# A hybrid MLA, SSD and RWKV kernel: one ct tile more, one h tile fewer, and RWKV row sums as single fp32 products

## The chip, the cores and the metric

The kernel runs on one core of a Trainium2 chip. The metric is the device time of one execution in microseconds (us); lower is better. Five engines work side by side, each through its own instructions in order: TensorE (PE; its weight loads are PEld), VectorE (DVE), ScalarE (ACT), GpSimd (POOL) and SyncE (SP, which here issues the DMAs). They wait for each other through semaphores.

## The reference

Two layers of a sequence model, batch 1, 1024 tokens of width 1024, fp32. Each layer normalises x with adaLN scale and shift, projects it to 4,680 columns, and feeds three branches: latent attention (MLA, 4 heads), a state space branch (SSD, 8 heads) and RWKV-7 (8 heads of 64). Their outputs are concatenated, projected and added to x under a gate.

```python
def reference(...):
    c_act = jax.nn.silu(c)
    for l in range(DEPTH):
        mod = c_act @ ada_w[l] + ada_b[l]
        shift, scale, gate = jnp.split(mod[:, None, :], 3, axis=-1)
        h = rms_norm(x, norm_w[l]) * (1.0 + scale) + shift
        (q_lat, ..., r, k, v, w_lo, a_lo, g_rwkv) = split_cols(h @ w_in[l], IN_SPLIT_SIZES)
        y_mla = mla_branch(...) * jax.nn.silu(g_mla)
        y_ssd = ssd_branch(...)
        y_rwkv = rwkv7_branch(...) * jax.nn.silu(g_rwkv)
        y = jnp.concatenate([y_mla, y_ssd, y_rwkv], axis=-1)
        x = x + gate * (y @ w_out[l])
    return rms_norm(x, final_norm_w)
```

In the RWKV branch two sums run over the 64 columns of each head, for every token:

```python
    kk = k * heads(k_k)
    kk = kk / jnp.maximum(jnp.sqrt(jnp.sum(kk * kk, axis=-1, keepdims=True)), 1e-12)
    ...
    y = y + jnp.sum(r * k * r_k.astype(f32), axis=-1, keepdims=True) * v
```

## The kernel before

Activations lie with features on the 128 partitions and 512 tokens (a half) along a row. A layer and a half make one stage: dense stages 0 to 3 are layer 0 half 0, layer 0 half 1, layer 1 half 0, layer 1 half 1. A dense stage makes h (make_h, L671) and projects it, 37 tiles of 128 columns (inproj, L705). For layer 1 it begins with the output projection of layer 0 (outproj, L1412), which also gives the new x; after the last stage two more output projections follow. Behind each dense stage come its consumers (L1625): RWKV in four head pairs, SSD, and attention.

Precise products are made of three reduced ones (fp32r): weights and activations are each split in a high and a low part, high in ScalarE, low in VectorE, and the products high-high, high-low and low-high are added up (split_w L534, split L1216, proj L692). A split activation takes two h tiles, a pair. Weights come through wr, wh and wl tiles.

Two tile pools matter here. **h** (N_H2 = 18 tiles of 128 x 512) holds x, the split h of a dense stage (8 pairs, 16 tiles), and in an output projection the 8 x tiles that are summed up and the split y tiles of a group. An output projection has three groups, one for each branch (y_split, L1403: 4 pairs a group). **ct** (N_CT = 4) holds what passes through: a y tile on its way from DRAM to its split (`ct<-yd`), an evacuated projection (evac L711, and L1430 in the first group), and rows of the adaLN matrix of the next layer (`ct<-in_ada_dram`, ada L610), which VectorE multiplies by the activated condition and adds up (`ac<-ct,cact,ac`, L631).

What sets the order is a planner. All instructions are recorded first (record, L257); order (L286) then places them with a table of costs and latencies: of those that could start, the one with the highest rank, which is what `plan.ahead` adds. The adaLN multiply-adds have rank 0 (PR_S, L61), their loads a high one (PR_L, L62), y loads and weight loads a high one (PR_D), and the consumers lie between. Tiles of a pool go to users in recorded order as they come free. The planner prices a product of at most 64 output rows at a fixed 103 ns (L230). So a change of a pool's size or of an instruction moves instructions on all engines.

The RWKV row sums: each head pair has one for the norm of kk (L788, two output rows, one for each head) and one for r k r_k (L834, 128 output rows). The left operand, bones, is 1 where two rows belong to the same head. With PQ = PB = 1 the squares (sq) or products (r) are split into fp32r parts in the tiles leafh and leafl, taken from the pool of b tiles, and two fp32r products with bones_r, a rounded copy of bones, are added up.

Of the kernel before, what the change touches and what calls it, by code (L numbers as in the profile page):

```python
# [10 lines left out]
F32R = mybir.dt.float32r  # L11
I32 = mybir.dt.int32
AF = mybir.ActivationFunctionType
# [4 lines left out]
P = 128  # L18
# [25 lines left out]
C_ID, C_MD, C_SM, C_BO, C_IF, C_SG, C_S4, C_M1 = 0, 128, 256, 768, 896, 897, 898, 902  # L44
NCST = 1030

N_H2, N_RT, N_RI, N_RQ, N_RL, N_CT, N_WR, N_WL, N_WH, N_B2 = 18, 5, 2, 2, 3, 4, 3, 3, 3, 17
N_BK, N_GG, N_BX, N_AR, N_BM, N_TT, N_RV, N_GT = 1, 2, 3, 1, 1, 2, 2, 2
RW_T = 0
N_EZ = 1  # L50
# [21 lines left out]
SG0 = "bbgggggg"  # L72
SBP, SBC, SCH = "ra", "ra", 2
SRB = "tf"
PQ = 1
PB = 1
PX = "b2"
WAT = "rv"
LOT = "rl"
# [318 lines left out]
def hybrid_layers_kernel(ctx: ExitStack, tc: tile.TileContext, A, out):  # L398
    nc = tc.nc
    plan = Plan(tc)  # L400
    V, S, G, PE, SP = (plan.engine(e, q) for e, q in ((nc.vector, "V"), (nc.scalar, "S"), (nc.gpsimd, "G"),
                                                      (nc.tensor, "P"), (nc.sync, "Q")))
    TQ, AL, AS, BL, BM, BS, EQ = SP, S, S, S, SP, S, SP

    cpool = ctx.enter_context(tc.tile_pool(name="cpool", bufs=1))
# [46 lines left out]
    def s1(n, tag=None, bufs=None):  # L452
        if bufs:
            return sm.tile([P, n], F32, name=nm("s"), tag=tag or f"s{n}", bufs=bufs)
        return sm.tile([P, n], F32, name=nm("s"), tag=tag or f"s{n}")

    def bank(tag):
        return ps.tile([P, HT], F32, name=nm("ps"), tag=tag, bufs=PSB[tag])
# [22 lines left out]
    bones = cst[:, C_BO:C_BO + 128]  # L481
# [17 lines left out]
    for e in range(2):  # L499
        SP.dma_start(cst[64:128, C_MD + 64 * e:C_MD + 64 * e + 64], A["cst"][64:128, C_MD + 64 * (1 - e):C_MD + 64 * (1 - e) + 64])  # L500
    SP.dma_start(mD1[64:128], A["cst"][64:128, C_MD:C_MD + 128])
    bones_r = cpool.tile([P, 128], F32R, name="bones_r")
    S.activation(bones_r, bones, AF.Copy)
    cth = s1(8)
    S.activation(cth, craw, AF.Tanh, scale=0.5)
    V.scalar_tensor_tensor(cth, cth, 1.0, craw, op0=ALU.add, op1=ALU.mult)
# [248 lines left out]
    def rwkv_a1(d, U, p, wa):  # L755
# [32 lines left out]
        pq = bank("ra")  # L788
        if PQ:
            hi, lo = WATS[PX](dt=F32R, leaf="leafh"), WATS[PX](dt=F32R, leaf="leafl")  # L790
# [13 lines left out]
    def rwkv_a2(d, p, u):  # L804
# [29 lines left out]
        pbn = bank("ra")  # L834
        if PB:
            hi, lo = WATS[PX](dt=F32R, leaf="leafh"), WATS[PX](dt=F32R, leaf="leafl")
# [917 lines left out]
```

## Time and profile before

| | |
|---|---|
| three runs | 1953.89 us median (1953.27 to 1957.49) |
| profiled execution | 1953.58 us, its span 1951.8 us |
| granted TensorE clock, mean | 0.975 |
| PE, DVE, ACT, POOL busy | 1825.9, 1619.7, 1205.9, 204.4 us |
| DMA | 341 MB, 175 GB/s |

A profile row groups instructions by line, engine, operation and tiles; every instruction is issued from L396, so rows are told apart by their tiles. `out<-in` names what is written and what is read, without buffer numbers. A product of plain fp32 operands makes two records of MATMUL, one of fp32r operands makes one. "Idle" in brackets is the engine's wait before an instruction, with what ended it. The granted clock is TensorE's share of its full rate (1.0 is 2.4 GHz, 0.5 is 1.2 GHz).

### The profile page before, as it was taken

Reading aid. Unit: us, or ns where it says so; the run is one execution under the profiler, and the core shown is the slowest. Engines: PE = TensorE matmul, PEld = TensorE weight load, DVE = VectorE, ACT = ScalarE, POOL = GpSimd, SP = SyncE. Lnnn points to the kernel's source line nnn. Section 1 sums busy time; section 2 is a strip of 40 time slices with the busy share of each in tenths; the row PEclk is TensorE's granted clock in tenths of the full one; section 3 lists DMA queues with packets and bytes.
Section 4 is the critical chain, followed back from the end, with each engine's and each line's share of the span. In section 5 each row is a group of like instructions: output and inputs, shape, how many; then the busy total and the mean of one; then the engine's idle time right before and its main releaser. Section 6 shows DMA issues by size and latency. Waiting matters only on the chain. (4 is left out here: it accounts for less than half of the span.)

```text
span 1951.8 us, 32300 instructions
## 1 busy us (share of the span) xinstructions
PE 1825.9 (94%) x10220; PEld 1460.7 (75%) x10220; DVE 1619.7 (83%) x4002; ACT 1205.9 (62%) x2520; POOL 204.4 (10%) x302
## 2 busy tenths in 40 slices
PE   5899997999999986989999999998999999999996
PEld 3677775888887764777778778787777877888884
DVE  7898898789897999787788978888788896978774
ACT  5566566676665655566657567675656557675652
POOL 2120011011010101020100001002010020001001
PEclk9999998999999986999999999999999999999997
DMA  7677666765658673744464665854456565753542
GB/s 248 219 201 200 182 198 190 225 200 164 190 152 212 195 205 102 238 132 114 122 165 133 157 203 171 272 170 141 131 146 177 157 203 171 246 162 100 183 144 73
DMA packets 273371, 341.31 MB, mean 175 GB/s; under 512 B 79152, under 2 KB 132016, under 8 KB 273200
## 3 DMA queue, kind: packets, MB, share of 16 engines
q1 hardware_dynamic: 273200, 339.25, 59.6%
q8 instruction: 81, 1.33, 0.3%
q14 instruction: 90, 0.74, 0.1%
HBM read 254.67 MB, written 84.47 MB: 174 GB/s over the span
## 5 line engine op out<-in xcount | busy, mean ns | idle before, releaser
L396 PE MATMUL ps<-h,wh 128*128 128x512 f32 x3136 | 1015.9, 407 | 35.3 <-ACT h L396 21.4
L396 PEld LDWEIGHTS ps<-h,wh 128*128 128x128 f32 x3136 | 581.2, 191 | 166.3 <-ACT h L396 26.8
L396 PE MATMUL ps<-h,wl 128*128 128x512 f32 x1568 | 590.1, 407 | 0.1
L396 PE MATMUL ps<-b,b 128*128 128x512 f32 (+4 forms) x1512 | 384.6, 356 | 10.5 <-DVE b L396 6.3
L396 ACT ACTIVATE wh<-wr 128x512 fp32r<-128x512 f32 (+1 forms) x398 | 246.4, 620 | 211.4 <-PE ps L396 164.3
L396 PEld LDWEIGHTS ps<-h,wl 128*128 128x128 f32 x1568 | 296.8, 191 | 56.7 <-issue 2.5
L396 DVE TENSOR_TENSOR wl<-wr,wh 128x512 fp32r<-128x512 f32 (+1 forms) x398 | 269.7, 680 | 59.4 <-ACT wh L396 41.1
L396 PEld LDWEIGHTS ps<-b,b 128*128 128x128 f32 (+1 forms) x1512 | 232.1, 184 | 67.6 <-DVE b L396 14.5
L396 ACT ACTIVATE b<-b 128x512 f32<-128x512 f32 (+3 forms) x222 | 136.9, 625 | 62.1 <-DVE b L396 25.6
L396 ACT ACTIVATE b<-ps 128x512 f32<-128x512 f32 (+3 forms) x201 | 99.4, 508 | 77.8 <-PE ps L396 73.6
L396 DVE TENSOR_TENSOR b<-b,b 128x512 fp32r<-128x512 f32 (+4 forms) x178 | 121.9, 690 | 18.4 <-ACT b L396 14.5
L396 DVE TENSOR_TENSOR rq<-rq,tmp 128x60 f32<-128x60 f32 (+24 forms) x496 | 109.1, 220 | 6.6
L396 DVE TENSOR_TENSOR tmp<-Q,rq 128x60 f32<-128x60 f32 (+24 forms) x496 | 104.3, 210 | 5.9
L396 ACT ACTIVATE ct<-ps 128x512 f32<-128x512 f32 x150 | 87.8, 588 | 24.1 <-PE ps L396 11.2
L396 PE MATMUL ps<-cst,b 128*128 128x128 f32 x452 | 81.6, 282 | 20.7 <-POOL b L396 15.0
L396 PEld LDWEIGHTS ps<-bx,gg 128*128 128x128 f32 x512 | 76.8, 194 | 32.2 <-DVE bx L396 15.8
L396 POOL COPY halo<-ct 128x3 f32<-128x3 f32 x84 | 28.6, 340 | 621.9 <-ACT ct L396 594.2
L396 PE MATMUL ps<-bx,gg 128*128 128x64 f32 x512 | 80.7, 273 | 9.2 <-DVE bx L396 7.6
L396 PEld LDWEIGHTS ps<-cst,b 128*128 128x128 f32 x452 | 58.4, 146 | 35.1 <-POOL b L396 15.0
L396 POOL TENSOR_TENSOR s<-s,nhalf 128x4 f32<-128x4 f32 (+1 forms) x34 | 54.0, 1591 | 258.1 <-DVE s L396 250.5
L396 DVE SCALAR_TENSOR_TENSOR h<-ps,md,h 128x512 f32<-128x512 f32 x72 | 53.5, 746 | 33.2 <-PE ps L396 32.7
L396 ACT ACTIVATE b<-ps,s,s 128x512 f32<-128x512 f32 (+2 forms) x96 | 63.9, 667 | 27.3 <-DVE s L396 24.3
(196 smaller groups left out, 2612.0 us busy)
## 6 DMA issues: line engine op xcount, KB each, us to landing
wr<-in_w_in_dram SPq DMA_DIRECT2D x282, 256.0 KB
U<-ct SPq DMA_DIRECT2D x84, 257.5 KB
wr<-in_w_out_dram SPq DMA_DIRECT2D x80, 256.0 KB
U<-ct SPq DMA_DIRECT2D x64, 256.0 KB
ct<-in_ada_dram SPq DMA_DIRECT2D x64, 256.0 KB
ri<-U SPq DMA_DIRECT2D x52, 257.5 KB
b<-accd SPq DMA_DIRECT2D x96, 128.0 KB
ct<-yd SPq DMA_DIRECT2D x48, 256.0 KB
```

What stands on the lines that cost most here:

```text
L396: o.fn(*o.args, **o.kw)
```

## The change

N_H2 goes from 18 to 17 and N_CT from 4 to 5. PQ and PB go from 1 to 0: the row sums are one plain fp32 product each, straight from sq or r with bones, without leafh, leafl and bones_r.

```diff
-N_H2, N_RT, N_RI, N_RQ, N_RL, N_CT, N_WR, N_WL, N_WH, N_B2 = 18, 5, 2, 2, 3, 4, 3, 3, 3, 17
+N_H2, N_RT, N_RI, N_RQ, N_RL, N_CT, N_WR, N_WL, N_WH, N_B2 = 17, 5, 2, 2, 3, 5, 3, 3, 3, 17
...
-PQ = 1
-PB = 1
+PQ = 0
+PB = 0
...
-    bones_r = cpool.tile([P, 128], F32R, name="bones_r")
-    S.activation(bones_r, bones, AF.Copy)
```

What the switch chooses between, in rwkv_a1 (rwkv_a2 has the same with r, bones and 128 output rows):

```python
        if PQ:
            hi, lo = WATS[PX](dt=F32R, leaf="leafh"), WATS[PX](dt=F32R, leaf="leafl")
            split(sq, hi, lo)
            mm(pq[0:2, :], bones_r[:, 0:128:64], hi, stop=False)
            mm(pq[0:2, :], bones_r[:, 0:128:64], lo, start=False)
        else:
            mm(pq[0:2, :], bones[:, 0:128:64], sq)
```

The order moves on every engine. The places below lie in the output projection of layer 0, half 0, at the change from its first group of y tiles (SSD) to its second (attention). First VectorE before: `h<-ct,h` is the low part of a y split, `ac<-ct,cact,ac` an adaLN multiply-add, rq, tmp and Q belong to the inversion of an RWKV matrix.

```order
L396 SCALAR_TENSOR_TENSOR h_2429<-ct_2427,h_2428 128x512
L396 TENSOR_TENSOR tmp_1807<-Q_1802,rq_1806 128x60
L396 SCALAR_TENSOR_TENSOR ac_1638<-ct_2394,cact,ac_1638 128x512
L396 TENSOR_TENSOR rq_1806<-rq_1806,tmp_1807 128x10x6
L396 SCALAR_TENSOR_TENSOR ac_1638<-ct_2401,cact,ac_1638 128x512
L396 TENSOR_TENSOR tmp_1807<-Q_1802,rq_1806 128x54
L396 SCALAR_TENSOR_TENSOR ac_1638<-ct_2408,cact,ac_1638 128x512
```

The multiply-adds of the last three adaLN rows stand behind the third split of the group (h_2429). VectorE in the changed kernel, from the first split of the same group (h_2390) to its last (h_2399):

```order
L396 SCALAR_TENSOR_TENSOR h_2390<-ct_2388,h_2389 128x512
L396 TENSOR_TENSOR rq_1777<-rq_1777,tmp_1778 128x19x4
L396 TENSOR_TENSOR wl_2410<-wr_2408,wh_2409 128x512
L396 TENSOR_TENSOR h_2379<-h_2379,ct_2381 128x512
L396 SCALAR_TENSOR_TENSOR h_2393<-ct_2391,h_2392 128x512
L396 TENSOR_TENSOR tmp_1778<-Q_1773,rq_1777 128x72
L396 TENSOR_TENSOR bm_1787<-bm_1787,s_1792 128x512
L396 SCALAR_TENSOR_TENSOR h_2396<-ct_2394,h_2395 128x512
L396 TENSOR_TENSOR rq_1777<-rq_1777,tmp_1778 128x18x4
L396 TENSOR_TENSOR wl_2415<-wr_2413,wh_2414 128x512
L396 SCALAR_TENSOR_TENSOR h_2399<-ct_2397,h_2398 128x512
```

The four splits stand close together, and the adaLN multiply-adds of this half all stand ahead of them. SP's queue, which issues the loads (yd is a y tile in DRAM), before:

```order
L396 DMA ct_2408<-in_ada_dram 128x512
L396 DMA b_2038<-rope_d 128x512
L396 DMA b_2039<-rope_d 128x512
L396 DMA wr_2461<-in_w_out_dram 128x512
L396 DMA ct_2421<-yd_583 128x512
L396 DMA b_2055<-in_w_q_dram 128x512
L396 DMA ct_2424<-yd_584 128x512
L396 DMA ct_2427<-yd_585 128x512
```

And in the changed kernel, where the last load of adaLN rows of that half is ct_2375:

```order
L396 DMA ct_2375<-in_ada_dram 128x512
L396 DMA qn_1998<-b_2028 128x512
L396 DMA ct_2388<-yd_582 128x512
L396 DMA wr_2413<-in_w_out_dram 128x512
L396 DMA ct_2391<-yd_583 128x512
L396 DMA qn_1999<-b_2033 128x512
L396 DMA b_2047<-in_w_v_dram 128x512
L396 DMA qn_2000<-b_2035 128x512
L396 DMA ct_2394<-yd_584 128x512
L396 DMA wr_2418<-in_w_out_dram 128x512
L396 DMA ct_2397<-yd_585 128x512
```

In the queue the two kinds of load stand in the same sequence; what moved is when VectorE frees the tiles that they wait for.

## Rows read from the trace of the kernel before

**Rows 1.** The page: busy us (share of the span) and instructions of each engine.

```profile
PE 1825.9 (94%) x10220; PEld 1460.7 (75%) x10220; DVE 1619.7 (83%) x4002; ACT 1205.9 (62%) x2520; POOL 204.4 (10%) x302
```

**Rows 2.** Busy time by stretch: start:end, length, each engine's busy us (records).

```profile
core 0: us, PE busy (x) PEld busy (x) DVE busy (x) ACT busy (x) POOL busy (x), PEclk, DMA share, GB/s
0.00:310.70 310.70, 271.81 (x1369) 210.30 (x1369) 267.44 (x660) 189.36 (x397) 45.74 (x71) 0.99 0.70 208
310.70:690.50 379.80, 360.53 (x2132) 291.60 (x2132) 330.46 (x854) 240.21 (x512) 37.21 (x66) 0.98 0.68 191
690.50:877.80 187.30, 156.85 (x876) 122.87 (x877) 163.67 (x388) 111.96 (x222) 22.40 (x23) 0.89 0.55 168
877.80:1951.80 1074.00, 1036.69 (x5846) 835.97 (x5844) 858.13 (x2102) 664.42 (x1391) 99.06 (x144) 0.98 0.55 161
...
80.00:310.70 230.70, 221.58 (x1172) 175.63 (x1170) 200.61 (x477) 144.96 (x289) 27.39 (x45) 0.99 0.73 206
335.00:675.00 340.00, 335.96 (x2023) 273.45 (x2022) 295.22 (x778) 222.68 (x478) 32.22 (x58) 0.99 0.68 190
735.00:785.00 50.00, 31.54 (x116) 22.17 (x114) 44.02 (x122) 29.04 (x55) 8.48 (x7) 0.69 0.34 105
```

**Rows 3.** Timeline of SP, 690 to 785 us: start, us, engine, out<-in, count.

```profile
710.67 0.33 SPq L396 DMA_DIRECT2D ct<-in_ada_dram  x1
721.04 0.33 SPq L396 DMA_DIRECT2D ct<-in_ada_dram  x1
748.41 0.33 SPq L396 DMA_DIRECT2D ct<-in_ada_dram  x1
755.92 0.32 SPq L396 DMA_DIRECT2D ct<-yd  x1
762.32 7.62 SPq L396 DMA_DIRECT2D ct<-yd  x2
776.80 0.42 SPq L396 DMA_DIRECT2D ct<-yd  x1
```

**Rows 4.** Timeline of VectorE, 735 to 792 us.

```profile
761.61 0.68 DVE L396 SCALAR_TENSOR_TENSOR h<-ct,h 128x512 fp32r<-128x512 f32 x1
768.90 0.68 DVE L396 SCALAR_TENSOR_TENSOR h<-ct,h 128x512 fp32r<-128x512 f32 x1
775.17 0.68 DVE L396 SCALAR_TENSOR_TENSOR h<-ct,h 128x512 fp32r<-128x512 f32 x1
775.91 0.74 DVE L396 SCALAR_TENSOR_TENSOR ac<-ct,cact,ac 128x512 f32<-128x512 f32 x1
776.71 0.74 DVE L396 SCALAR_TENSOR_TENSOR ac<-ct,cact,ac 128x512 f32<-128x512 f32 x1
777.91 0.74 DVE L396 SCALAR_TENSOR_TENSOR ac<-ct,cact,ac 128x512 f32<-128x512 f32 x1
```

**Rows 5.** Timeline of TensorE, 728 to 792 us: idle before it in brackets.

```profile
767.55 0.57 PE L396 MATMUL ps<-h,wh 128*128 128x512 f32 x1 [3.31 <-ACT h L396]
769.64 0.79 PE L396 MATMUL ps<-h,wh 128*128 128x512 f32 x1 [1.52 <-DVE h L396]
```

**Rows 6.** Groups by form: busy us, mean ns | idle before; what the change removes.

```profile
L396 DVE TENSOR_TENSOR leafl<-rt,leafh 128x512 fp32r<-128x512 f32 x32 | 22.0, 687 | 2.5 <-ACT leafh L396 2.1
L396 ACT ACTIVATE leafh<-rt 128x512 fp32r<-128x512 f32 x32 | 20.0, 626 | 3.0 <-DVE rt L396 2.6
L396 PE MATMUL ps<-leafh,bones_r 128*128 128x512 f32 x16 | 6.9, 430 | 0.4 <-ACT wh L396 0.4
L396 PE MATMUL ps<-leafh,bones_r 128*2 128x512 f32 x16 | 6.8, 427 | 0.0
```

**Rows 7.** Timeline of TensorE, 1900 to 1908 us: starts of back-to-back products.

```profile
1902.36 1.09 PE L396 MATMUL ps<-h,wh 128*128 128x512 f32 x4
1903.28 0.40 PE L396 MATMUL ps<-h,wl 128*128 128x512 f32 x1
...
1905.34 0.59 PE L396 MATMUL ps<-b,b 128*128 128x256 f32 x2
1905.77 0.27 PE L396 MATMUL ps<-cst,b 128*128 128x128 f32 x1
```

**Rows 8.** Groups by form: small fp32 products, two records each.

```profile
L396 PE MATMUL ps<-rq,ar 32*32 32x32 f32 x512 | 18.7, 193 | 0.0
L396 PE MATMUL ps<-gg,bk 128*128 128x128 f32 x512 | 72.2, 283 | 8.1 <-DVE bk L396 3.5 <-ACT bx L396 2.6 <-issue 0.8
```

## Prediction

> **What bounds the kernel now.** I read the page's busy shares first: TensorE is busy 94% of the span, VectorE 83%, ScalarE 62% [rows 1]. Shares over a whole program hide its stages, so the next view is the busy time in four stretches that the program's own landmarks cut [rows 2]. A ends where VectorE begins to normalise the x of dense stage 1 (310.7 us). B is dense stage 1 with the work of the first two consumers. C runs from the first split y tile of layer 0's output projection (690.5 us) to the first normalised tile of layer 1 (877.8 us). D is the rest. In B and D TensorE works 95% and 97% of the time; from 335 to 675 us it is 336.0 of 340 us. There time is TensorE's work, and what the other engines do is cover. C is the exception: 156.9 busy of 187.3 us, the granted clock 0.89, and in its middle (735 to 785 us) 31.5 of 50 us at a granted 0.69. So 30.5 us of C are idle TensorE, and part of the rest ran at the lower of the two clock levels. The projection products are there to fill C; why don't they?
>
> The DMA queue and VectorE in that stretch say why [rows 3, 4]. SP issued adaLN rows into ct tiles at 710.67, 721.04 and 748.41 us. The multiply-adds that read them (ac<-ct,cact,ac) have the lowest rank and ran at 775.91, 776.71 and 777.91 us. Three of four ct tiles lay locked. The y tiles of the projection's second group went through the one that was left: issued at 755.92, split at 761.61 to 762.29, the next issued at 762.32, split at 768.90 to 769.58, the next after that, split at 775.17. Each y tile waits until the one before has been read: 6 to 7 us a turn. TensorE waits for it: 3.31 us for ScalarE's h and 1.52 us for VectorE's [rows 5].
>
> **The change, part by part.** *Row sums.* Each of the 32 removes one ScalarE copy (0.626 us), one VectorE subtract (0.687 us) and two fp32r products of 512 columns, and adds one plain fp32 product of 512 columns [rows 6]. Four fp32r products back to back start 0.92 us apart (1902.36 to 1903.28), 0.23 each; a plain fp32 product of 256 columns is two records and takes 0.43 us to the next start (1905.34 to 1905.77) [rows 7]. By columns 512 take 0.86. The 2-column sums cost as much as the 128-column ones (427 against 430 ns [rows 6]). So a sum costs 0.86 - 0.46 = 0.40 us more of TensorE: 32 x 0.40 = 12.8 us, of which 30 sums, 12.0 us, lie outside C in the new order. The bounds are 0 (all of them in idle time) and 12.8; B, D and the part of A that has sums (80 to 310.7 us: 221.6 of 230.7 us busy [rows 2]) are nearly full, so I take the upper. The 20.0 us of ScalarE and 22.0 us of VectorE that go [rows 6] are counted at nothing outside C, since TensorE's own work hides them; it shortens the chain copy, subtract, product, product by about a microsecond a head pair, which counts where TensorE waits. If it were TensorE that had slack, this part alone would be a gain.
>
> Beside that, from a page: the Trainium skill (FP8 and Floating Point Precision, TensorE Precision Notes) says that true fp32 takes four passes through the array. By that a sum would cost 4 x 0.23 = 0.92 and 32 of them 14.7 us more instead of 12.8; the row (0.43 for half the columns) is a little under it. It speaks against the change.
>
> *One ct tile more.* It gives C's ring a second free tile while three are locked, so a load can be under way while the tile before is split. The new order goes further: the adaLN multiply-adds stand ahead of the second group's splits (first and second order pieces), so that the locked tiles are free again too. Between the first and last split of that group VectorE had 47 instructions; now 10. In the whole of C VectorE has 294 instructions where it had 387, TensorE 624 where it had 696, with the same projection work (291 products against 288).
>
> What C then needs: VectorE 294 x 163.67/387 = 124 us [rows 2]. TensorE 156.85 us now, less the small products that moved out, less what it lost to the clock. The moved ones are 138 records, 64 of them of the 32 x 32 kind (18.7/512 = 0.037 us); the 128 x 128 kind has 0.141 [rows 8]: bounds 5 and 19 us, and I take 7, near the small kind. The clock: a mean of 0.69 over 735 to 785 us is 62% of it at half rate; that share of 31.5 busy us is 20, which at full rate would be 10. So TensorE needs 157 - 7 - 10 = 140 us, and with 4% idle (B and D have 5 and 3%) C takes 146 us. The bounds are 130 (VectorE's 124 with the same idle) and 180 (187.3 - 7, nothing gained).
>
> *One h tile fewer.* An output projection holds 8 x tiles and 8 split y tiles; of 18 two were left, a whole split pair ahead, and of 17 one. At each change of group (nine in the four projections) the second tile of a pair may have to wait. The nearest rows are the split itself, 0.68 us on VectorE [rows 4], and the wait for a late pair, 3.31 us [rows 5]; the lower bound is nothing, as the new order puts three of that group's four splits within 7 instructions. I take 0 at the point and keep 9 x 0.68 = 6 us for the range. The x loads of stage 1 are all but one issued after the H tiles come free; before, all but two: one load more of 0.4 us issue at 310 us, nothing.
>
> *The sum*, against the profiled execution (span 1951.8, 1953.6 in all, 0.3 under the median): A, B and D 1951.8 - 187.3 = 1764.5; plus sums 12.0; plus the work moved out of C 7.0; plus C 146; that is 1929.5, and 1.8 us around the span: **1931 us**.
>
> **Rivals.** *VectorE paces B and C.* It is busy 494 of their 567 us [rows 2], and its share in C is higher than TensorE's. For it: if VectorE was the limit, freeing ct tiles gives TensorE nothing to do sooner. Against it: TensorE waited for a split whose tile had not been loaded. In the new order the two stretches hold 1187 VectorE instructions instead of 1240; 53 x 0.40 = 21 us less, the sums cost 12.8 on TensorE outside: 1953.6 + 12.8 - 21 = 1945.
>
> *The change doesn't do what it says: the fifth tile fills with adaLN rows too.* The loads run ahead as far as tiles allow, eight in a row for a half, and their readers stay last in rank. Then C keeps its 187 us, the sums are paid in full, and the time is 1953.6 + 12.8 = 1966, slower. For it: the same rule of ranks; against it: the place of the multiply-adds in the new order. C has to shrink by more than 12.8 us before there is any gain; that is the point from which it decides.
>
> *The h pool opens the gap that the ct pool closed.* At every group change TensorE waits for the second tile of the pair. At 2.5 us a change (between 0.68 and 3.31) nine cost 22: 1931 + 22 = 1953, no change; above 2.9 us each it is slower. The Trainium skill (Perfetto Trace Analysis, Optimization Strategy) reads the same gap repeating on the engine that should be full as too few buffers; C's gaps of 6 to 7 us fit it for ct, and for h no repeated gap is in these rows. Its result would be this rival's.
>
> **How the numbers follow.** A measurement of this kernel tells about 0.2%, 4 us, from no change. The forecast, C between 130 and 166 us, 0.58; VectorE paces, 1945, 0.15; the ring stays locked, 1966, 0.18; the h gap, 1953, 0.09. Faster is the forecast and most of the second: 0.71; slower the third and part of the fourth: 0.22; the rest, 0.07, within 0.2%. The range: low with C at 130, 1764.5 + 19 + 130 + 1.8 = 1915, a little lower for small gains elsewhere, 1912; the high end takes in the second and fourth rival and reaches into the third, 1962. The forecast's own range is 1913 to 1949.
>
> **What would show it.** Right: in the trace after, 32 pairs of plain fp32 records at 0.43 us a record; TensorE's work up by about 13 us; C at 135 to 160 us with a granted clock near 0.97; y loads of the second group issued within some 5 us instead of 21; the wait for ScalarE's h there gone. Wrong: C as long as before, with adaLN rows lying in four tiles; or gaps of 2 to 3 us in front of split pairs at each group change; or VectorE above 95% over B with TensorE idle in front of the first y tile. A sum at 0.46 us (two passes a product) would put 12 us more on the gain.

## The result, and the profile after

The changed kernel takes 1939.07 us (median of four, 1937.37 to 1940.78) against 1954.22 of the kernel before beside it: 0.9923 of the time, interval 0.9901 to 0.9945. The forecast was 1931 us in a range of 1912 to 1962. So the time fell as forecast, by 15 us instead of 23. The page's first line, against [rows 1]:

```profile
PE 1828.5 (94%) x10220; PEld 1446.4 (75%) x10220; DVE 1593.1 (82%) x3970; ACT 1190.4 (61%) x2487; POOL 202.0 (10%) x302
```

The span fell from 1951.8 to 1937.4 us. TensorE is busy 2.6 us longer, and idle 108.9 us instead of 125.9, so in this count the whole gain is idle time that went. (The busy time holds two changes that nearly cancel: by the prediction's estimates the sums add 12.8 us, and the fuller clock in C gives back 10.) Where the idle time went is read from the same four stretches as in [rows 2], cut at the same landmarks (start:end, length, each engine's busy us and records, then granted clock, DMA share, GB/s); the last row is the same 50 us as in [rows 2]:

```profile
0.00:321.30 321.30, 280.95 (x1390) 213.96 (x1390) 272.15 (x673) 191.26 (x397) 47.16 (x74) 0.99 0.69 207
321.30:727.30 406.00, 380.16 (x2273) 302.30 (x2272) 348.21 (x895) 254.53 (x536) 39.55 (x63) 0.97 0.65 183
727.30:866.30 139.00, 133.42 (x747) 106.13 (x746) 119.77 (x296) 89.80 (x183) 16.58 (x20) 1.00 0.65 206
866.30:1937.40 1071.10, 1034.01 (x5815) 823.99 (x5814) 853.02 (x2111) 654.77 (x1373) 98.66 (x145) 0.99 0.55 161
675.00:727.30 52.30, 41.67 (x255) 34.59 (x253) 47.55 (x97) 30.96 (x58) 6.08 (x6) 0.84 0.67 209
735.00:785.00 50.00, 48.43 (x234) 37.87 (x235) 48.30 (x119) 35.84 (x69) 5.27 (x5) 1.00 0.83 270
```

C is 139.0 us long instead of 187.3, its idle time 5.6 instead of 30.5, its clock 1.00 instead of 0.89. In 735 to 785 us TensorE is busy 48.4 us where it was 31.5, and the clock is full where it was 0.69. But B grew by 26 us. In its last 52.3 us TensorE is idle for 10.6 us, at a clock of 0.84 (fifth row). That hole is not new. The kernel before was idle for 7.5 us in the last 15.5 us of its B:

```profile
675.00:690.50 15.50, 8.00 (x55) 6.11 (x53) 13.04 (x38) 7.09 (x17) 0.81 (x3) 0.85 0.83 237
```

So of B's 6.6 us more idle time some 3 us lie at its end, and the rest at its start and in its middle. The DMA queue in C, against [rows 3] (start, us, engine, out<-in, count):

```profile
754.97 0.38 SPq L396 DMA_DIRECT2D ct<-yd  x1
758.81 0.42 SPq L396 DMA_DIRECT2D ct<-yd  x1
764.21 0.38 SPq L396 DMA_DIRECT2D ct<-yd  x1
765.13 0.42 SPq L396 DMA_DIRECT2D ct<-yd  x1
```

VectorE there, against [rows 4]:

```profile
756.35 0.75 DVE L396 SCALAR_TENSOR_TENSOR ac<-ct,cact,ac 128x512 f32<-128x512 f32 x1
759.62 0.74 DVE L396 SCALAR_TENSOR_TENSOR ac<-ct,cact,ac 128x512 f32<-128x512 f32 x1
766.40 0.69 DVE L396 SCALAR_TENSOR_TENSOR h<-ct,h 128x512 fp32r<-128x512 f32 x1
768.36 0.69 DVE L396 SCALAR_TENSOR_TENSOR h<-ct,h 128x512 fp32r<-128x512 f32 x1
769.71 0.69 DVE L396 SCALAR_TENSOR_TENSOR h<-ct,h 128x512 fp32r<-128x512 f32 x1
771.05 0.69 DVE L396 SCALAR_TENSOR_TENSOR h<-ct,h 128x512 fp32r<-128x512 f32 x1
```

The adaLN multiply-adds run ahead of the splits; the four y loads of the second group are issued within 10 us where they took 21, the four splits run within 5 us. TensorE's waits for an h there, against [rows 5]:

```profile
739.06 0.74 PE L396 MATMUL ps<-h,wh 128*128 128x512 f32 x2 [0.45 <-DVE h L396]
774.18 0.73 PE L396 MATMUL ps<-h,wh 128*128 128x512 f32 x2 [0.53 <-DVE h L396]
```

The waits of 3.31 and 1.52 us are gone. They were only a part of the hole before: of TensorE's 18 us of idle time between 735 and 785 us, waits for an h ended 6.1 us. Most of the rest ended with work of the consumers, for instance (before):

```profile
738.78 1.12 PE L396 MATMUL ps<-bx,gg 128*128 128x64 f32 x4 [2.16 <-DVE bx L396]
747.20 1.12 PE L396 MATMUL ps<-cst,s 128*128 128x128 f32 x4 [2.67 <-POOL s L396]
```

Nearly all of this is as forecast (the y loads were to be issued within some 5 us, and took 10). Read by itself, this trace would seem to prove that the fifth ct tile freed the ring. The experiments say otherwise.

The row sums in the changed kernel, against [rows 7], first one with 128 output columns, then one with two, each with the start of what follows it on TensorE:

```profile
356.36 1.02 PE L396 MATMUL ps<-rt,cst 128*128 128x512 f32 x2
357.22 0.94 PE L396 MATMUL ps<-bx,Ez 128*128 128x128 f32 x7
...
395.20 1.02 PE L396 MATMUL ps<-rt,cst 128*2 128x512 f32 x2
396.15 0.44 PE L396 MATMUL ps<-cst,b 128*128 128x128 f32 x2
```

A sum is two records. The 128-column one takes 0.86 us to the next start, the two-column one 0.95; forecast was 0.86 for both. It is the same in the whole trace: all 16 two-column sums take 0.95 us, whatever stands behind them. Of the 128-column ones 12 take 0.85 to 0.97 us; in the other four another product starts between the two records.

### The profile page after: what moved, and what is told of

Read it like the earlier page. It is cut to its first block, busy times and chain, and to the rows that moved or that the text cites. A ratio compares the mean times of both kernels' runs of the same rounds, so it can differ in the third digit from the quotient of the medians.

```text
span 1937.4 us, 32242 instructions
## 1 busy us (share of the span) xinstructions
PE 1828.5 (94%) x10220; PEld 1446.4 (75%) x10220; DVE 1593.1 (82%) x3970; ACT 1190.4 (61%) x2487; POOL 202.0 (10%) x302
## 4 chain that ended last, share of the span: by engine, by line
PE 68%; DVE 13%; DMA 7%; ACT 6%; issue 3%; SPq 1%; POOL 1%; POOLq 0%; ACTq 0%; DVEq 0%
PE ps L396 68%; DVE h L396 3%; DMA b<-accd 2%; ACT b L396 2%; DVE wl L396 2%; DVE b L396 1%; DVE bx L396 1%; SPq L396 1%; DVE s L396 1%; DMA U<-ct 1%; DMA wr<-in_w_in_dram 1%; DVE rq L396 1%; ACT wh L396 1%; ACT ct L396 1%; DVE tmp L396 1%
## 5 line engine op out<-in xcount | busy, mean ns | idle before, releaser
L396 PE MATMUL ps<-h,wh 128*128 128x512 f32 x3136 | 1015.5, 407 | 38.3 <-DVE h L396 16.7
L396 PE MATMUL ps<-b,b 128*128 128x512 f32 (+4 forms) x1512 | 374.8, 354 | 6.0 <-DVE b L396 3.1
L396 PEld LDWEIGHTS ps<-b,b 128*128 128x128 f32 (+1 forms) x1512 | 227.1, 181 | 62.3 <-ACT b L396 11.9
L396 POOL COPY halo<-ct 128x3 f32<-128x3 f32 x84 | 33.2, 396 | 707.9 <-ACT ct L396 707.7
L396 ACT ACTIVATE b<-ps,s,s 128x512 f32<-128x512 f32 (+2 forms) x96 | 63.9, 667 | 42.7 <-DVE s L396 37.8
L396 DVE TENSOR_REDUCE s<-ps 128x1 f32<-128x512 f32 (+4 forms) x114 | 65.1, 574 | 13.0 <-PE ps L396 11.4
```

Of the source, the lines that this page charges most:

```text
L396: o.fn(*o.args, **o.kw)
```

## The experiments

Idle TensorE time (length less busy in the stretches A to D of the prediction, from the same kind of rows, cut in each kernel at its own landmarks) sorts the kernels better than the total does. Ratios are to the kernel before on the same chip: 1954 us beside the changed kernel, 1949 to 1950 us beside all others. The idle times of the first two rows come from the chip with 1954 us. frozen_keep, which has the order of before, shows 6.6 us less idle time in all than the row of before, so a difference of that size between the first two rows and the others is not to be read.

| kernel | ratio (interval) | idle A | B | C | D | all, us |
|---|---|---|---|---|---|---|
| before | 1 | 38.9 | 19.3 | 30.5 | 37.3 | 125.9 |
| changed kernel | 0.9923 (0.9901 to 0.9945) | 40.4 | 25.8 | 5.6 | 37.1 | 108.9 |
| sums_only | 1.0012 (1.0000 to 1.0024) | 36.6 | 27.3 | 9.4 | 39.7 | 113.0 |
| pools_only | 0.9957 (0.9942 to 0.9972) | 39.6 | 13.5 | 29.5 | 34.5 | 117.1 |
| h17_sums | 1.0008 (0.9993 to 1.0023) | 36.9 | 34.2 | 10.8 | 35.9 | 117.7 |
| plan4_real5 | 1.0002 (0.9992 to 1.0012) | 36.0 | 32.4 | 10.4 | 35.5 | 114.3 |
| frozen_keep | 1.0061 (1.0044 to 1.0077) | 35.5 | 16.7 | 29.3 | 37.8 | 119.3 |
| frozen_drop | 1.0033 (1.0018 to 1.0048) | 35.4 | 18.4 | 28.5 | 36.1 | 118.3 |
| before_rank | 1.0255 (1.0224 to 1.0287) | 43.2 | 20.6 | 42.4 | 57.3 | 163.6 |
| pools_rank | 1.0180 (1.0158 to 1.0202) | 43.2 | 11.0 | 45.0 | 53.1 | 152.2 |
| before_vv | 0.9987 (0.9972 to 1.0002) | 39.3 | 19.3 | 30.6 | 34.4 | 123.5 |
| before_pv | 0.9999 (0.9982 to 1.0016) | 36.6 | 29.7 | 16.9 | 38.7 | 121.9 |
| after_vv | 1.0003 (0.9985 to 1.0021) | 39.2 | 27.8 | 9.9 | 37.4 | 114.3 |
| after_pv | 1.0004 (0.9990 to 1.0019) | 40.4 | 28.2 | 11.2 | 40.2 | 120.0 |

### The two halves of the change, apart

sums_only: the kernel before with the switches at 0 (and without the copy bones_r, as in the change).

```diff
-PQ = 1
-PB = 1
+PQ = 0
+PB = 0
```

> The kernel before with the row sums as single plain fp32 products and nothing else (18 h tiles, 4 ct tiles). Theory A (the fifth ct tile closes the hole in C): the ring of four stays, C keeps about 187 us and the sums are paid, 1953.6 + 12.8 = 1966 us (1958 to 1970). Theory O (what counts is the place of the adaLN multiply-adds in the planned order; here they stand ahead of the second group's splits although there are only four ct tiles): the hole closes as in the changed kernel, C about 140 us, time 1934 to 1946. Theory V (the work taken from VectorE and ScalarE is the gain): 1933 to 1945 as well, with C's hole still there.

pools_only: the kernel before with the pools alone.

```diff
-N_H2, ..., N_CT, ... = 18, 5, 2, 2, 3, 4, 3, 3, 3, 17
+N_H2, ..., N_CT, ... = 17, 5, 2, 2, 3, 5, 3, 3, 3, 17
```

> The kernel before with 17 h and 5 ct tiles, row sums as before (split, two fp32r products). Theories A and O: C shrinks as in the changed kernel and the sums are not paid, 1939 - 13 = 1926 us (1920 to 1932). Theory V: nothing gained, 1950 to 1957.

Measured: sums_only 1.0012, pools_only 0.9957. Both are misses for theory A, which wanted +13 us of the one and -28 us of the other. The other theories miss too: O has the short C of sums_only right but not its time (1934 to 1946 us), V has neither time, and none of them gives the 1940 us of pools_only. B and C of sums_only, with four ct tiles:

```profile
320.20:722.10 401.90, 374.63 (x2229) 295.56 (x2228) 343.43 (x889) 247.22 (x525) 42.12 (x66) 0.96 0.65 191
722.10:869.30 147.20, 137.80 (x755) 109.38 (x756) 122.32 (x293) 93.23 (x189) 15.73 (x17) 0.98 0.56 175
```

And C of pools_only, with five, and its 50 us from 735 on:

```profile
678.70:874.60 195.90, 166.44 (x942) 130.09 (x942) 171.96 (x408) 119.06 (x238) 23.75 (x25) 0.93 0.58 183
...
735.00:785.00 50.00, 39.63 (x175) 30.28 (x175) 48.52 (x123) 30.91 (x54) 7.89 (x6) 0.83 0.42 134
```

The hole closes without the tile (C 147.2 us, idle 9.4) and stays with it (195.9 us, idle 29.5). In pools_only the fifth tile was filled too. SP's ct loads from 692 us on (one of y between them left out):

```profile
692.00 0.40 SPq L396 DMA_DIRECT2D ct<-in_ada_dram  x1
...
697.01 0.33 SPq L396 DMA_DIRECT2D ct<-in_ada_dram  x1
702.95 0.38 SPq L396 DMA_DIRECT2D ct<-in_ada_dram  x1
708.81 0.60 SPq L396 DMA_DIRECT2D ct<-in_ada_dram  x1
715.38 0.35 SPq L396 DMA_DIRECT2D ct<-in_ada_dram  x1
725.10 0.38 SPq L396 DMA_DIRECT2D ct<-in_ada_dram  x1
754.19 0.32 SPq L396 DMA_DIRECT2D ct<-yd  x1
```

and the multiply-adds on VectorE:

```profile
721.69 0.74 DVE L396 SCALAR_TENSOR_TENSOR ac<-ct,cact,ac 128x512 f32<-128x512 f32 x1
750.25 0.74 DVE L396 SCALAR_TENSOR_TENSOR ac<-ct,cact,ac 128x512 f32<-128x512 f32 x1
753.42 0.74 DVE L396 SCALAR_TENSOR_TENSOR ac<-ct,cact,ac 128x512 f32<-128x512 f32 x1
```

Six rows loaded and one read by 725 us: five tiles locked until 750 us, and the next y tile is issued at 754.19, behind the next reads. That is the prediction's third case (the fifth tile fills too), but in pools_only, not in the changed kernel. pools_only is still 8 us faster than before. Its trace has 5.8 us less idle time in B and 2.8 less in D, together not far above the 6.6 us that frozen_keep shows without a new order, and no single place that explains the 8 us. It is one order, and no second order with these pools and the old sums was run, so its cause stays open.

### Four ct tiles in the changed kernel, and a fifth without a new order

h17_sums: the changed kernel with N_CT at 4.

> The changed kernel with 4 ct tiles instead of 5 (17 h tiles). Theory A: C's hole is back, 1960 to 1970 us. Theory O: in its order the adaLN multiply-adds stand ahead of the second group's splits, so no hole, 1935 to 1946. The h pool opens gaps at group changes (rival of the prediction): waits of 2 to 3 us in front of the second pair of a group, and 6 to 20 us over the kernel with 18 h tiles and 4 ct tiles.

plan4_real5: the order of h17_sums, the same on every engine, with a fifth tile in the pool. The planner is told 4 (a part of one line of order):

```diff
-... bufs=t.bufs or t.tag_meta.bufs, ...
+... bufs=dict(ct=4).get(t.tag.split("_")[0]) or t.bufs or t.tag_meta.bufs, ...
```

> The order of the kernel with 17 h and 4 ct tiles, kept word for word on every engine (the planner is told 4), with a fifth ct tile really there: it differs from h17_sums only in that loads may start a tile earlier. Theory A, in the part that a load can be under way while the tile before is split: 5 to 20 us faster than h17_sums. Theory O: the tile by itself does little, within 4 us of h17_sums.

Measured 1.0008 and 1.0002: the tile by itself gives 1.6 us between the medians, and the intervals overlap. C's hole is closed in both (idle 10.8 and 10.4), B's is larger (34.2 and 32.4). Theory O is right about the tile and about the short C, and wrong about the time of h17_sums (1935 to 1946 us). Against sums_only the 17 h tiles cost nothing that can be told (1.0008 and 1.0012), but these two kernels have different orders, so a cost of a few us could hide in the difference. Theory A's miss again: C needs no fifth tile to be short.

### The row sums priced in a frozen order

Both keep the order of before on every engine. frozen_keep puts the plain product where the high product stood; frozen_drop leaves the splits out as well:

```diff
 mm(pq[0:2, :], bones_r[:, 0:128:64], hi, stop=False)
 mm(pq[0:2, :], bones_r[:, 0:128:64], lo, start=False)
+plan.ops[-2].alt = lambda: nc.tensor.matmul(pq[0:2, :], bones[:, 0:128:64], sq, start=True, stop=True)
+plan.ops[-1].alt = lambda: None
...
```

(Where an instruction has an `alt`, that is issued in its place, after the planning. frozen_drop has, behind the split, `plan.ops[-2].alt = plan.ops[-1].alt = lambda: None` too; the other sum is done alike.)

> The order of the kernel before, kept word for word on every engine; only where a row sum's high product stood there is now one plain fp32 product of the unsplit operand, and the low product is left out. The splits on ScalarE and VectorE still run, and nobody reads their results. So it prices the product alone. Theory P (the prediction's term: TensorE is full where the sums stand, 0.40 us each by columns, up to 0.49 by the slots of the changed kernel): 13 to 16 us over before. Rival (the extra product lies in TensorE's idle time): 0 to 5 us over before.

> As frozen_keep, with the 32 ScalarE copies and 32 VectorE subtracts left out as well: still the order of before, so it prices the work that the change takes from ScalarE and VectorE (20.0 and 22.0 us). Theory P: within 4 us of frozen_keep. Theory V (that work paces B and C): 8 to 20 us faster than frozen_keep, so at or below before. If both frozen kernels stand some 13 us over before, while sums_only, planned anew, stood 2 us over it, what gave back the difference is the new order.

Measured: frozen_keep, 1.0061, is 11.9 us over before (8.6 to 15.0), so 0.37 us a sum. frozen_drop, 1.0033, is 6.4 us over before, 5.5 us less; the two intervals overlap a little (1.0044 to 1.0077, 1.0018 to 1.0048). The page's first line of each:

```profile
PE 1839.2 (94%) x10220; PEld 1458.1 (74%) x10220; DVE 1618.6 (83%) x4002; ACT 1207.3 (62%) x2520; POOL 206.1 (11%) x302
```

```profile
PE 1837.6 (94%) x10220; PEld 1459.6 (75%) x10220; DVE 1601.9 (82%) x3970; ACT 1190.6 (61%) x2488; POOL 204.5 (10%) x302
```

TensorE's busy time is 13.3 and 11.7 us over the 1825.9 of before; C keeps its hole in both (29.3 and 28.5 us idle). Theory P holds for the product: its 13 to 16 us overlap the interval, the rival's 0 to 5 do not. Of the 42 us of other engines' work that the change removes, 5.5 came through, a little more than P's 4 and less than V's 8. The expectation that both would stand some 13 us over before holds for frozen_keep; frozen_drop stands half as high. Planned anew (sums_only) the same work stands 2.3 us over before; the other 4 us of frozen_drop went with the new order, though its interval (1.0018 to 1.0048) and that of sums_only (to 1.0024) touch.

### Is the rank of the multiply-adds the cause of the hole?

before_rank is the kernel before, pools_rank is pools_only, with one number changed:

```diff
-PR_S = 0
+PR_S = 2000000
```

> The kernel before with the rank of the adaLN multiply-adds raised from 0 to 2,000,000, which puts them ahead of the consumers' work: four ct tiles, 18 h tiles, row sums as before. Theory O (the hole is ct tiles locked by multiply-adds of the lowest rank): idle TensorE in C falls from 30.5 to about 10 us and the half-rate time with it, and the time by 10 to 25 us, without a fifth tile. Rival (the hole is VectorE's work as a whole, and moving some of it ahead only moves the hole): within 4 us of before.

> The kernel with 17 h and 5 ct tiles and the old row sums (pools_only), with the same raised rank. There C still had 29.5 us of idle TensorE, and five ct tiles locked by adaLN rows. Theory O: C's idle falls to some 10 us, 10 to 20 us faster than pools_only, so 20 to 30 us faster than before. Rival (VectorE): within 4 us of pools_only.

Measured 1.0255 and 1.0180: both 44 to 50 us slower than the kernel they were made from, a miss of both theories in the time. In before_rank the second and third group's splits begin at 729.7 and 749.2 us (before: 761.6 and 807.0), so the ring was freed. Then:

```profile
800.00:830.00 30.00, 22.40 (x104) 17.54 (x104) 26.36 (x63) 17.55 (x34) 9.12 (x10) 0.84 0.41 138
830.00:860.00 30.00, 18.70 (x101) 13.37 (x102) 12.38 (x24) 10.30 (x19) 0.00 (x0) 0.50 0.27 74
```

TensorE is idle for 27 of the 80 us from 780 to 860. From 830 to 860 TensorE is busy 18.7 of 30 us, all of it at the lower clock level, and VectorE only 12.4: neither engine is full there. The hole moved, as the rival expected. A reading that fits: the projection's products are what TensorE has to fill the consumers' chains with, and spent early, they are missing later; then the locked tiles delayed the projection but were not the reason that there is a hole. No run shows this by itself, since the raised rank moves the multiply-adds of the whole program and gives another order everywhere. Of the 50.6 us by which the span is longer than before, 12.9 are busy time, 20.0 more idle time in D and 11.9 in C.

### How much is the order alone?

The planner's table has latencies in ns; one of them is raised by 1 ns, which tells the planner nothing but makes ties fall otherwise. The same two edits are made in both kernels (vv in the first line, pv in the second):

```diff
-... "VV": 127 ...
+... "VV": 128 ...
...
-... "PV": 196 ...
+... "PV": 197 ...
```

> The kernel before, planned anew: one latency in the planner's table (VectorE to VectorE) is 128 ns instead of 127, which says nothing of the chip but lets the order come out otherwise from the middle of the program on; pools and row sums as before. Theory C (pools and row sums decide the time): within 4 us of before. Theory L (a part of the 15 us is how an order happens to fall): 4 to 12 us away, in either direction.

> The kernel before, with another latency of the planner's table (TensorE to VectorE) at 197 ns instead of 196; the order differs on every engine, and the adaLN multiply-adds stand ahead of the second group's splits here. Theory C: within 4 us of before. Theory L: 4 to 12 us away. If the place of the multiply-adds alone closed the hole in C (first form of theory O): 8 to 15 us faster.

> The changed kernel with the planner's latency VectorE to VectorE at 128 ns instead of 127: same pools, same row sums, another order. Theory C: within 4 us of the changed kernel, 0.990 to 0.995 of before. Theory L: spread over 0.987 to 1.000 of before.

> The changed kernel with the planner's latency TensorE to VectorE at 197 ns instead of 196. Theory C: 0.990 to 0.995 of before. Theory L: spread over 0.987 to 1.000 of before; three multiply-adds stand between the second group's splits here, so by the first form of theory O a hole as in the kernel before would be back in C.

Measured: before_vv 0.9987 and before_pv 0.9999, as theory C wanted; after_vv 1.0003 and after_pv 1.0004, as theory L wanted (a hair past its 1.000). So each theory fails on one of the two kernels. With the same pools and the same sums, two of three orders gain nothing over the kernel before. C of before_pv, of after_vv and of after_pv:

```profile
707.40:882.10 174.70, 157.81 (x868) 122.12 (x867) 150.21 (x360) 110.34 (x218) 20.16 (x22) 0.90 0.55 170
```

```profile
714.60:878.10 163.50, 153.59 (x885) 121.86 (x885) 138.25 (x340) 103.11 (x211) 17.16 (x20) 0.96 0.56 172
```

```profile
732.80:868.90 136.10, 124.89 (x678) 98.60 (x678) 114.52 (x278) 84.21 (x172) 15.90 (x18) 0.96 0.58 183
```

after_pv has C as short as the changed kernel (136.1 us) and no gain, though three multiply-adds stand between its second group's splits; before_pv has none there, and C shrank by 12.6 us, and no gain either: B grew by 18.5. So a short C, the sign on which the forecast rested, does not tell a fast kernel. What the table does show: the six kernels whose order was planned with plain sums (five orders, since plan4_real5 has that of h17_sums) have less idle time in C (5.6 to 11.2 us) than the four with split sums and the old rank (16.9 to 30.6), and in B 25.8 to 34.2 against 13.5 to 29.7. In the plain ones the first y split comes at 714.6 to 740.5 us, in the split ones at 678.7 to 707.4: the projection begins later. That C then has the fill that it lacked is a reading; no run moves the projection's start alone. B's larger idle time takes back a part of what C gains, and the sums' own work another part.

The changed kernel has the least idle time of all (108.9 us, against 114.3 and 120.0 of after_vv and after_pv). The others do not lose in one place. after_pv and sums_only reach the end of C at 868.9 and 869.3 us, nearly with the changed kernel (866.3), and then take 9 us longer over D (1080.1 and 1080.5 against 1071.1). after_vv is 11.8 us late at the end of C and 2.8 faster in D. Which placements of the changed kernel make the difference stays open. Two cautions belong to it: it was timed beside the kernel before on another chip than these (before there 1954 us, here 1949), and was not timed again beside after_vv and after_pv.

## Why the prediction was right, and where it was not

*The time.* 1939 against 1931 forecast. The sum missed by 8 us in two terms that partly cancel: C took 139.0 us, not 146 (7.0 less), and A, B and D took 1798.4 us, not 1783.5 (14.9 more). Of those 14.9, 7.1 are busy TensorE (1695.1 us against 1669.0 before, 26.1 more where 19.0 were forecast) and 7.8 are idle: 6.6 more in B, 1.5 more in A, 0.2 less in D. The term "work moved out of C", 7 us from bounds of 5 to 19, was too small. C lost 129 records and 23.4 busy us, and without the 10 counted for the clock that leaves 13; A, B and D grew by 14 busy us beyond the 12.0 of their sums. So some 13 to 14 us moved. That the other stretches would get 7.8 us more idle time when C lost 24.9 was in no term.

*The row sums.* Right: 12.8 forecast, 11.9 (8.6 to 15.0) measured with the order held. One part was too small: the prediction priced the two-column sums like the others, and they took 0.95 us instead of 0.86, 1.4 us for the 16. The Trainium skill (FP8 and Floating Point Precision, TensorE Precision Notes) says four passes, by which an estimate is 14.7 us; the interval holds both.

*The removed ScalarE and VectorE work at nothing.* Somewhat wrong: 5.5 us in the frozen order, near the edge of the noise. The VectorE rival took 21 us for less VectorE work, which is too much; that its 1945 us lies a little nearer to the measured time than the forecast is no support for it, since in 735 to 785 us VectorE went from 44.0 to 48.3 us busy while TensorE gained 17, so it had not been full.

*The ct tile.* The step that failed is "it gives C's ring a second free tile ... the new order goes further". What the order does was seen rightly in the rows, and most signs that the prediction named came true in the trace of after (TensorE's busy time rose by 2.6 us and not by 13, and the y loads took 10 us and not 5). But the cause was wrong for C: four tiles close its hole as well (sums_only, h17_sums), five do not close it by themselves (pools_only's C), a fifth tile in a fixed order gives 1.6 us (plan4_real5), and freeing the tiles by rank made the kernel slower. The gaps of 6 to 7 us that the prediction names are turns of the ring; TensorE itself waited 3.31, 1.52 and 1.24 us for split y tiles, a third of its idle time in the hole. None of these kernels with four tiles has the changed kernel's time, though, so that the fifth tile lets the planner find faster orders is not ruled out: of three orders with it and plain sums one was faster, of two with four tiles none. The Trainium skill (Perfetto Trace Analysis, Optimization Strategy) reads a repeated gap as a sign that may mean too few buffers; here the gap went with no buffer more and stayed with one more. The measurement decides.

*The h tile.* Right in that no gap opened at the group changes: the longest wait of TensorE for a split there is 0.81 us. Its price is not settled to a few us (1.0008 against 1.0012, in two orders).

*The chances.* "Faster" at 0.71 rested on a mechanism that the runs do not show to carry a gain by itself. The case that was missing among the rivals: the new order is one draw of many, and sums and pools together are worth about nothing in two of three draws. That this draw is the fast one could not be read from a shorter C (after_pv has it too), so that the time fell at all was in part luck.

## What to carry to other kernels

Where a planner orders everything, hold the order still to price an edit (replace instructions after the planning), and plan again with a meaningless change of 1 ns to see how far orders scatter; a gain inside that scatter cannot be put down to the edit. A ring that is locked ahead of a starved engine is a delay, but not yet a cause: ask what the engine will run on after its fill has come earlier. Add up idle time over the whole neighbourhood of a hole, since a hole that closes in one stretch may have moved into the next.

## What the runs showed of the hardware

A plain fp32 product of 512 columns with two output columns took 0.95 us to the next start, 16 times of 16; with 128 output columns it took 0.85 or 0.86 in seven of the 12 that nothing interrupted, and 0.93 to 0.97 in the other five. Fewer output columns were no cheaper here. From 830 to 860 us in before_rank the granted clock was at the lower level (1.2 GHz) without a break, and TensorE was busy 62% of that time; in the changed kernel's C, busy 96%, it was at the upper level (2.4 GHz) throughout. So a hole cost twice here: of the 50 us from 735 on, before did 31.5 busy us at 0.69 where after did 48.4 at 1.00.
